# Mixture-of-experts stage of an encoder layer: the experts' instructions in a written order, eight split pairs, and the experts' inputs in another part of the memory

## The chip, the cores and the metric

The kernel runs on one core of a Trainium2 chip. The metric is the device time of one execution in microseconds (us). The kernel before takes 2306.76 us, the median of three runs (2303.48 to 2307.94).

A core has a matrix engine (TensorE, PE in the profile; PEld is its weight load), a vector engine (DVE), a scalar engine (ACT), GpSimd (POOL), and SyncE (SP), which here only issues loads. Each runs its own list of instructions in order and waits for the others through semaphores. Sixteen DMA engines move data between HBM and the on-chip memory SBUF (128 partitions). Matmul results go to PSUM.

## The reference

One layer: a token mixer (attention and a gated linear recurrence), then experts. The change touches only the experts, which end the program:

```python
def expert_choice_ffn(h, w_router, w_gate, w_up, w_down):
    ...
    affinity = jax.nn.softmax(logits, axis=-1)
    top_w, top_idx = lax.top_k(affinity.transpose(0, 2, 1), cap)
    xe = jax.vmap(lambda hb, ib: hb[ib])(h, top_idx)
    hid = jax.nn.silu(jnp.einsum('becd,edf->becf', xe, w_gate)) * jnp.einsum('becd,edf->becf', xe, w_up)
    ye = jnp.einsum('becf,efd->becd', hid, w_down) * top_w[..., None].astype(h.dtype)
    combine = lambda yb, ib: jnp.zeros((S, D), h.dtype).at[ib.reshape(-1)].add(yb.reshape(-1, D))
    return jax.vmap(combine)(ye, top_idx)
```

There are 16 experts. Each takes 128 of 1024 tokens of width 1024 and has a hidden width of 2048. All is float32.

## The kernel before

**Splitting.** A float32 product is made of three fp32r products. Every operand is split into a high part (a cast on ACT, line 89) and the rest (a subtraction on DVE, line 90), and `hi*hi + hi*lo + lo*hi` is summed in PSUM. The helper is `split`.

**Units.** The experts' weights come in units of 128 rows by 1024 columns (512 KB). A unit is loaded by SP (line 56) into a raw buffer (`er`), split into a pair `eh`, `el`, and used by six matmuls of 128 x 512. An expert has 48 units: for each of two halves of the hidden width, 8 of the gate matrix, 8 of the up matrix, 8 of the down matrix. In all there are 768 units and 4608 such matmuls.

**Matmuls.** For gate and up (`wide`, lines 1255 to 1257, into the PSUM tiles `pg`) the stationary operand is a 128 x 128 slice of the expert's transposed input, `xh` or `xl`; the moving operand is `eh` or `el`. For down (`down`, lines 1218 to 1220, into `py`) it is a slice of the transposed hidden rows, `hh` or `hl`.

**Between them.** `pick` (lines 1198 to 1206) makes the list of an expert's tokens: a one-hot tile `oh` on DVE, eight small matmuls, `idx` and `tw` on DVE, and a gather `xg` by a GpSimd DMA. `trans` turns a tile by PE (line 1184) and splits it: the input `xg` in eight pieces on ACT (line 1188, `xh`) and DVE (line 1189, `xl`), the hidden rows `hd` in two (`hh`, `hl` on lines 89 and 90). Silu is on ACT (line 1273), its product with up on DVE (line 1284), the weighting of the result (`ye`, line 1225) on DVE, and a GpSimd DMA adds it to the output (line 1226).

**What sets the order.** The order in which each engine's instructions stand is found by a scheduler that goes by priorities and its own estimates; the code is written gate, down of the half before, up. Nothing in the experts' part fixes it, except that a few splits are held back at the start.

**Buffers.** There are 26 raw buffers (7 `er`, 16 of a pool shared with earlier stages, 3 `er3`) and four more tiles (`ahead`) that are lent to loads before their own use starts. There are five pairs (`EB`), so a split waits until PE has used the unit five before it. SBUF is filled from both sides: pool `exr`, `side="right"`, holds `er`, `er3`, `ye` and the inputs `xh`, `xl`; pool `ex` on the left holds `hh`, `hl`, `xg`, `hd`; `ex1` holds the pairs. In the built program, counted in KB from the start of a partition: the pairs at 86 to 126, `hh` and `hl` at 146 to 154, `xh` and `xl` at 170 to 186. In PSUM, `pg` has banks 2 to 5, `py` 6 and 7; `s` of lines 928 to 930 has 2 to 4. In an earlier stage, lines 928 to 930, the stationary weights lie at 82 to 114 and the moving operands `och`, `ocl` at 134 to 198.

Of the kernel before, what the change touches and what calls it, by code (L numbers as in the profile page):

```python
# [21 lines left out]
P = 128  # L22
D = 1024
# [14 lines left out]
def trunk(ctx, tc, t, out, dbg=None):  # L38
# [16 lines left out]
    def load(dst, src):  # L55
        return nc.sync.dma_start(dst, src)
# [90 lines left out]
    def h4(name, shape, dt=F32R):  # L147
        return hpool.tile(shape, dt, name=name, tag="H", bufs=16)
# [993 lines left out]
    psE = ctx.enter_context(tc.tile_pool(name="psE", bufs=1, space=PSUM))  # L1142
    wg_, wu_, wd_ = (t[n].rearrange("l e a b -> (l e) a b") for n in ("w_exp_gate", "w_exp_up", "w_exp_down"))

    NR = ER + 16 + E3
    cnt = [0]
    held, ahead = [], []

    def eunit(src):
        shape = [P] + list(src.shape)[1:]  # L1150
        j = cnt[0] if cnt[0] < NR else cnt[0] - len(ahead)
        c = j % NR
        if NR <= cnt[0] < NR + len(ahead):
            raw = ahead[cnt[0] - NR]
        elif c < ER:
            raw = exr.tile(shape, F32, name="er", bufs=ER)
        elif c >= ER + 16:
            raw = exr.tile(shape, F32, name="er3", tag="er3", bufs=E3)
        else:
            raw = h4("er2", shape, F32)  # L1160
        if not NR <= cnt[0] < NR + len(ahead):
            load(raw, src)
        cnt[0] += 1
        hi = ex1.tile(shape, F32R, name="eh", bufs=EB)
        lo = ex1.tile(shape, F32R, name="el", bufs=EB)
        with ExitStack() as es:
            if cnt[0] <= EB:
                es.enter_context(tc.issue_after(first5[-2]))
                es.enter_context(tc.issue_after(first5[-1]))
            if 3 < cnt[0] <= 24:  # L1170
                es.enter_context(tc.issue_after(held[0]))
            if EB < cnt[0] <= 24:
                es.enter_context(tc.issue_after(held[8]))
            split(raw, hi, lo, nc.gpsimd if cnt[0] <= 3 else None)
        return hi, lo

    def trans(src, n, tag):
        pool = exr if tag == "x" else ex
        hi = pool.tile([P, n, P], F32R, name=tag + "h", tag=tag + "h", bufs=2)
        lo = pool.tile([P, n, P], F32R, name=tag + "l", tag=tag + "l", bufs=2)  # L1180
        for g in range(0, n, 4):
            p = psE.tile([P, 4, P], F32, name="tp", bufs=2)
            for c in range(4):
                nc.tensor.transpose(p[:, c], src[:, (g + c) * P:(g + c + 1) * P], ident)
            if tag == "x":
                for c in range(4):
                    k = g + c
                    held.append(nc.scalar.activation(hi[:, k], p[:, c], AF.Identity, bias=mcT[:, k:k + 1], scale=1.0).ins)  # L1188
                    nc.vector.scalar_tensor_tensor(lo[:, k], p[:, c], mcT[:, k:k + 1], hi[:, k].bitcast(F32),  # L1189
                                                   op0=ALU.add, op1=ALU.subtract)  # L1190
            else:
                split(p, hi[:, g:g + 4], lo[:, g:g + 4])
        return hi, lo

    def pick(e):

        oh = ex.tile([P, NT, P], BF16, name="oh", bufs=1)
        nc.vector.tensor_tensor(oh, slots[:, None, :].to_broadcast([P, NT, P]),
                                slot[:, :, e:e + 1].to_broadcast([P, NT, P]), ALU.is_equal)
        pi = psE.tile([P, 512], F32, name="tp", bufs=2)  # L1200
# [4 lines left out]
        xg = ex.tile([P, D], F32, name="xg", tag="xg", bufs=2)  # L1205
# [4 lines left out]
    def down(e, fp, hTs, py, ks):  # L1210

        for kk in ks:
            hh, hl = hTs[kk // 4]
            r = kk % 4
            wh, wl = eunit(dunit(e, (fp * 8 + kk) * P))
# [5 lines left out]
        if fp == 1 and ks[-1] == 7:  # L1221
            ye = exr.tile([P, D], F32, name="ye", tag="ye", bufs=YB)
            for n in range(2):
                sl = slice(n * 512, (n + 1) * 512)
                nc.vector.scalar_tensor_tensor(ye[:, sl], py[:, n], tw[:, e:e + 1], g2b[:, sl], op0=ALU.mult, op1=ALU.mult)
            nc.gpsimd.indirect_dma_start(out=out, out_offset=bass.IndirectOffsetOnAxis(ap=idx[:, e:e + 1], axis=0),
                                         in_=ye, in_offset=None, compute_op=ALU.add)

    def gunit(e, w, fp, k):
        return w[e, k * P:(k + 1) * P, fp * 1024:(fp + 1) * 1024].rearrange("(k p) n -> p k n", p=P)  # L1230
# [1 line left out]
    def dunit(e, r0):  # L1232
        return wd_[e, r0:r0 + P].rearrange("(k p) n -> p k n", p=P)


    for tag, n, src in (("ye", YB, dunit(0, 2 * P)), ("xh", 2, dunit(0, 3 * P)), ("xl", 2, dunit(0, 4 * P)),
                        ("xg", 2, dunit(0, 5 * P))):
        a = (exr if tag in X2 else ex).tile([P] + list(src.shape)[1:], F32, name="ahead", tag=tag, bufs=n)
        load(a, src)
        ahead.append(a)  # L1240

    with tc.high_priority(300):
        xparts = trans(pick(0), KT, "x")

    def wide(e, w, fp, parts, between=None):

        xh, xl = parts
        ps = [psE.tile([P, 512], F32, name="pg", bufs=4) for _ in range(2)]
        for k in range(KT):
            if between and k == 4:  # L1250
                between()
            wh, wl = eunit(gunit(e, w, fp, k))
            for n in range(2):
                sl = slice(n * 512, (n + 1) * 512)
                nc.tensor.matmul(ps[n], xh[:, k], wh[:, 0, sl], start=k == 0, stop=False)  # L1255
                nc.tensor.matmul(ps[n], xh[:, k], wl[:, 0, sl], start=False, stop=False)  # L1256
                nc.tensor.matmul(ps[n], xl[:, k], wh[:, 0, sl], start=False, stop=k == KT - 1)  # L1257
        return ps

    def turned(hds):  # L1260
        return [trans(hd, 4, "h") for hd in hds]

    pend = None
    py = None
    for e in range(NE):
        mine = xparts
        for fp in range(2):
            turn = []
            gs = wide(e, wg_, fp, mine, (lambda: turn.extend(turned(pend[2]))) if pend else None)
            acts = []  # L1270
            for n in range(2):
                hd = ex.tile([P, 512], F32, name="hd", tag="hd", bufs=3)
                nc.scalar.activation(hd, gs[n], AF.Silu)
                acts.append(hd)
            last = e == NE - 1 and fp == 1
            if fp == 0 and e + 1 < NE:
                xg = pick(e + 1)
            if pend and not last:
                if pend[1] == 0:
                    py = psE.tile([P, 2, 512], F32, name="py", bufs=1)  # L1280
                down(pend[0], pend[1], turn, py, range(8))
            us = wide(e, wu_, fp, mine)
            for n in range(2):
                nc.vector.tensor_tensor(acts[n], acts[n], us[n], ALU.mult)
            if fp == 1 and e + 1 < NE:
                xparts = trans(xg, KT, "x")
            if last:
                py = psE.tile([P, 2, 512], F32, name="py", bufs=1)
                down(pend[0], pend[1], turn, py, range(4))
                t0 = trans(acts[0], 4, "h")  # L1290
                down(pend[0], pend[1], turn, py, range(4, 8))
                down(e, 1, [t0, trans(acts[1], 4, "h")], py, range(8))
            pend = (e, fp, acts)
# [43 lines left out]
```

## Time and profile before

| | us |
|---|---|
| median of 3 runs | 2306.76 |
| the profiled execution, its own time | 2305.64 |
| its span, first to last instruction | 2303.80 |
| first matmul of the experts (line 1255) starts | 1132.36 |
| last DMA of the experts is issued (line 1226) | 2293.95 |
| between the two | 1161.59 |

The page gives, per engine, the busy time over the whole span. The views by stretch of time (windows), by waits, and the timelines are read below. A busy PE is not a PE at its peak, since matmuls overlap in the record: how fast it goes is read from the distance between the starts of two matmuls, called the pitch here.

### The profile page before, as it was taken

What the parts mean: (1) busy time and instruction counts of PE and PEld (TensorE: products, weight loads), DVE (VectorE), ACT (ScalarE), POOL (GpSimd) and SP (SyncE); (2) the same over time, 40 slices, a digit from 0 to 9 for tenths busy, and PEclk for the clock granted to TensorE, in tenths of its full rate; (3) what the DMA queues carried; (4) which work ended last, traced back from release to release, by engine and by line L of the source; (5) the groups of instructions that cost most, each with busy time, mean ns of one, the idle gap of its engine ahead of it and who ended that gap; (6) DMA issues with size and microseconds to landing.
All of it is one profiled execution on the core that took longest, in us unless ns stands there. A gap on an engine that the chain in (4) does not pass through costs nothing.

```text
span 2303.8 us, 30740 instructions
## 1 busy us (share of the span) xinstructions
PE 2150.1 (93%) x10518; PEld 1718.9 (75%) x10518; DVE 1868.5 (81%) x2601; ACT 1383.3 (60%) x2051; POOL 363.9 (16%) x341
## 2 busy tenths in 40 slices
PE   5998888999999999998499999999999999999997
PEld 4775665788888768897377877778777777777776
DVE  7699998588756465728899999999888898888886
ACT  4657666544433122224477777777777776777675
POOL 5247666000000000005200000000100000000000
PEclk9999999999999999999699999999999999999999
DMA  8111111422231885458589999999999999999992
GB/s 290 58 40 38 38 37 33 142 89 78 97 96 65 257 280 177 136 181 284 181 325 385 365 360 362 369 381 372 338 352 360 367 352 364 354 347 369 355 337 85
DMA packets 208246, 546.84 MB, mean 237 GB/s; under 512 B 19589, under 2 KB 75429, under 8 KB 208090
## 3 DMA queue, kind: packets, MB, share of 16 engines
q1 hardware_dynamic: 185242, 495.08, 59.4%
q0 software_dynamic: 8416, 29.41, 4.5%
q10 hardware_dynamic: 14432, 20.39, 2.5%
q8 instruction: 82, 1.34, 0.2%
q14 instruction: 74, 0.61, 0.1%
HBM read 503.80 MB, written 41.01 MB: 236 GB/s over the span
## 4 chain that ended last, share of the span: by engine, by line
PE 68%; DVE 14%; issue 7%; DMA 5%; ACT 4%; POOL 1%; SPq 0%; ACTq 0%; POOLq 0%; DVEq 0%
PE pg L1256 9%; PE pg L1257 9%; PE pg L1255 9%; PE py L1219 5%; PE py L1220 5%; PE py L1218 4%; DVE Tl L90 3%; PE g L208 2%; PE g L210 2%; PE s L711 2%; PE g L209 2%; DMA wr<-in_ada_w 2%; DVE el L90 2%; DVE mx L567 2%; ACT eh L89 1%
## 5 line engine op out<-in xcount | busy, mean ns | idle before, releaser
L90 DVE TENSOR_TENSOR el<-er,eh 128x1024 fp32r<-128x1024 f32 x761 | 898.1, 1220 | 66.3 <-ACT eh L89 54.6
L89 ACT CAST eh<-er 128x1024 fp32r<-128x1024 f32 x764 | 780.2, 1052 | 144.2 <-PE pg L1257 102.4
L1256 PE MATMUL pg<-el,xh 128*128 128x512 f32 x1024 | 412.0, 403 | 8.6 <-DVE el L90 7.5
L1257 PE MATMUL pg<-eh,xl 128*128 128x512 f32 x1024 | 402.1, 397 | 0.3
L1255 PE MATMUL pg<-eh,xh 128*128 128x512 f32 x1024 | 367.6, 399 | 3.6 <-ACT xh L1188 3.4
L1256 PEld LDWEIGHTS pg<-el,xh 128*128 128x128 f32 x1024 | 192.5, 188 | 65.0 <-DVE el L90 21.7
L1255 PEld LDWEIGHTS pg<-eh,xh 128*128 128x128 f32 x1024 | 192.4, 188 | 53.5 <-ACT xh L1188 7.8
L1257 PEld LDWEIGHTS pg<-eh,xl 128*128 128x128 f32 x1024 | 191.3, 188 | 48.2 <-DVE xl L1189 7.4
L1219 PE MATMUL py<-el,hh 128*128 128x512 f32 x512 | 202.8, 396 | 7.6 <-DVE el L90 7.6
L1218 PE MATMUL py<-eh,hh 128*128 128x512 f32 x512 | 201.5, 394 | 0.8 <-ACT eh L89 0.5
L1220 PE MATMUL py<-eh,hl 128*128 128x512 f32 x512 | 199.8, 390 | 0.0
L208 PE MATMUL g<-hTh,wh 128*128 128x512 f32 x448 | 179.8, 401 | 5.0 <-ACT wh L89 2.9
L210 PE MATMUL g<-hTh,wl 128*128 128x512 f32 x448 | 179.6, 401 | 0.3 <-DVE wl L90 0.2
L209 PE MATMUL g<-hTl,wh 128*128 128x512 f32 x448 | 178.8, 399 | 0.0
L1206 POOL DMA_INDIRECT xg<-d_h,idx x16 | 29.1, 1821 | 804.4 <-DVE idx L1203 678.2
L90 DVE TENSOR_TENSOR Tl<-E,Th 128x512 fp32r<-128x512 f32 x128 | 134.2, 1071 | 2.2 <-ACT Th L89 2.1
L638 POOL TENSOR_TENSOR sum<-sum,E 128x512 f32<-128x512 f32 x84 | 128.2, 1526 | 25.4 <-ACT E L632 20.4
L1219 PEld LDWEIGHTS py<-el,hh 128*128 128x128 f32 x512 | 96.0, 188 | 35.7 <-DVE el L90 15.6
L1218 PEld LDWEIGHTS py<-eh,hh 128*128 128x128 f32 x512 | 96.1, 188 | 25.1 <-ACT eh L89 5.1
L228 ACT ACTIVATE stg<-g 128x512 f32<-128x512 f32 (+1 forms) x78 | 45.1, 578 | 109.3 <-PE g L210 70.1
L1220 PEld LDWEIGHTS py<-eh,hl 128*128 128x128 f32 x512 | 96.2, 188 | 18.8
L90 DVE TENSOR_TENSOR wl<-wr,wh 128x1024 fp32r<-128x1024 f32 x56 | 68.6, 1227 | 43.9 <-ACT wh L89 43.9
(336 smaller groups left out, 3912.3 us busy)
## 6 DMA issues: line engine op xcount, KB each, us to landing
er<-in_w_exp_gate SPq DMA_DIRECT2D x256, 512.0 KB
er<-in_w_exp_up SPq DMA_DIRECT2D x256, 512.0 KB
er<-in_w_exp_down SPq DMA_DIRECT2D x252, 512.0 KB
wr<-in_w_in SPq DMA_DIRECT2D x42, 512.0 KB
wr<-in_ada_w SPq DMA_DIRECT2D x32, 512.0 KB
d_sg<-stg ACTq DMA_DIRECT2D x32, 256.0 KB
sg<-d_sg SPq DMA_DIRECT2D x16, 512.0 KB
d_zq<-stg ACTq DMA_DIRECT2D x24, 256.0 KB
```

The source lines that it names most:

```text
L89: first = nc.scalar.copy(hi, src)
L90: (eng or nc.vector).tensor_tensor(lo, src, hi.bitcast(F32), ALU.subtract)
L208: nc.tensor.matmul(p, wh[:, k], xT(hTh, n, k), start=k == 0, stop=False)
L209: nc.tensor.matmul(p, wh[:, k], xT(hTl, n, k), start=False, stop=False)
L210: nc.tensor.matmul(p, wl[:, k], xT(hTh, n, k), start=False, stop=k == KT - 1)
L638: (nc.vector if j == NH - 1 else nc.gpsimd).tensor_tensor(a, acc, E, ALU.add)
L1218: nc.tensor.matmul(py[:, n], hh[:, r], wh[:, 0, sl], start=fp == 0 and kk == 0, stop=False)
L1219: nc.tensor.matmul(py[:, n], hh[:, r], wl[:, 0, sl], start=False, stop=False)
L1220: nc.tensor.matmul(py[:, n], hl[:, r], wh[:, 0, sl], start=False, stop=fp == 1 and kk == 7)
L1255: nc.tensor.matmul(ps[n], xh[:, k], wh[:, 0, sl], start=k == 0, stop=False)
L1256: nc.tensor.matmul(ps[n], xh[:, k], wl[:, 0, sl], start=False, stop=False)
L1257: nc.tensor.matmul(ps[n], xl[:, k], wh[:, 0, sl], start=False, stop=k == KT - 1)
```

## The change

The experts' part is written as a list (`script`) of units and of actions between them, and an in-order block keeps that order on PE, DVE and ACT. Gate comes first, then up, then the down of the half before. The turn of the hidden rows stands before the fifth up unit, `pick` and the turn of the next input before the fifth down unit. The split of a unit is put on ACT and DVE right after the unit whose pair it takes over (`ensure`).

The memory is laid out anew. Raw buffers: 26 for the first 26 units, then a ring of 19 (3 `er`, 16 shared); one tile is lent instead of four. The seven `er3` tiles serve as raw buffers once, then hold three further pairs, so there are eight. `xh`, `xl` move to the left pool: they now lie at 136 to 152 KB, `hh`, `hl` at 160 to 168, the three further pairs at 170 to 198. `hd` has four buffers instead of three, `xg` one instead of two.

```diff
-    ER, E3, EB, YB = 7, 3, 5, 1
+    EB, MORE, YB = 5, 3, 1
+    RAW = dict(er=3, er3=7)
...
+    TAGS = ["er"] * 3 + ["H"] * 16 + ["er3"] * 7
+    RING, PAIR = ["er"] * 3 + ["H"] * 16, "er3"
...
+    def pair_tag(j):
+        return PAIR if j >= PAIRS0 and (j - PAIRS0) % (EB + MORE) >= EB else None
...
-        pool = exr if tag == "x" else ex
-        hi = pool.tile([P, n, P], F32R, name=tag + "h", tag=tag + "h", bufs=2)
-        lo = pool.tile([P, n, P], F32R, name=tag + "l", tag=tag + "l", bufs=2)
+        hi = ex.tile([P, n, P], F32R, name=tag + "h", tag=tag + "h", bufs=2)
+        lo = ex.tile([P, n, P], F32R, name=tag + "l", tag=tag + "l", bufs=2)
...
+        if tag == "x":
+            for k in range(n):
+                held.append(nc.scalar.activation(hi[:, k], ps[k // 4][:, k % 4], AF.Identity, bias=mcT[:, k:k + 1],
+                                                 scale=1.0).ins)
+            for k in range(n):
+                nc.vector.scalar_tensor_tensor(lo[:, k], ps[k // 4][:, k % 4], mcT[:, k:k + 1], hi[:, k].bitcast(F32),
+                                               op0=ALU.add, op1=ALU.subtract)
...
+    for h in range(NH2):
+        e, fp = divmod(h, 2)
+        more = e + 1 < NE
+        for k in range(KT):
+            wide_unit(e, wg_, h, (h, 0), k)
+        act(lambda h=h: silu(h))
+        if more and not fp:
+            act(lambda e=e: set_(ohs, e + 1, lambda: onehot(e + 1)))
+        for k in range(KT):
+            if k == 4:
+                if h:
+                    act(lambda h=h: (turn(h - 1, 0), turn(h - 1, 1)))
...
+            wide_unit(e, wu_, h, (h, 1), k)
+        act(lambda h=h: gated(h))
+        for kk in range(8) if h else ():
+            if kk == 4 and more:
+                if fp:
+                    act(lambda e=e: set_(xparts, e + 1, lambda: trans(xgs[e + 1], KT, "x")))
+                else:
+                    act(lambda e=e: set_(xgs, e + 1, lambda: pick(e + 1, ohs[e + 1])))
...
+            down_unit(h - 1, kk)
...
+    def ensure(done):
+
+        while len(parts_) < len(srcs) and before[len(parts_)] < done:
+            parts_.append(eparts(eload(srcs[len(parts_)]), len(parts_)))
...
+    with in_order(ET.PE, ET.DVE, ET.Activation):
+        j = 0
+        for z, run in script:
+            if z is None:
+                run()
+            else:
+                ensure(j)
+                run(*parts_[j])
+                j += 1
```

On ACT before, in the second half of the experts, the casts of units (`eh<-er`) and the split of the turned hidden rows (`hh<-tp`, which needs PE's transposes) stand like this:

```order
L89 CAST eh<-er_17615 128x1024
L89 CAST eh<-er_17627 128x1024
L89 CAST eh<-er_17671 128x1024
L89 CAST eh<-er_17683 128x1024
L89 CAST eh<-er_17695 128x1024
L89 CAST hh<-tp 128x512 x2
L89 CAST eh<-er_17707 128x1024
L89 CAST eh<-er 128x1024 x6
L1273 ACTIVATE hd<-pg 128x512 x2
```

The cast ahead of `hh` takes a pair that PE frees three units before the transposes. Now, at a like place of ACT:

```order
L1294 ACTIVATE hd<-pg 128x512 x2
L89 CAST eh<-er_19855 128x1024
L89 CAST eh<-er_19869 128x1024
L89 CAST eh<-er_19881 128x1024
L89 CAST eh<-er_19893 128x1024
L89 CAST hh<-tp 128x512 x2
L89 CAST eh<-er_19923 128x1024
L89 CAST eh<-er_19935 128x1024
```

Silu (`hd<-pg`) stands where gate ends, `hh` four casts later, where PE's transposes stand four units later: the cast ahead of `hh` takes the pair of the last but one unit before the transposes.

On DVE before, where the next expert's input is split (`xl`), its pieces alternate with the rests of units (`el`):

```order
L1189 SCALAR_TENSOR_TENSOR xl<-tp,mcT,xh 128x128
L90 TENSOR_TENSOR el<-er_16736,eh 128x1024
L1189 SCALAR_TENSOR_TENSOR xl<-tp,mcT,xh 128x128
L90 TENSOR_TENSOR el<-er_16748,eh 128x1024
L1189 SCALAR_TENSOR_TENSOR xl<-tp,mcT,xh 128x128
L90 TENSOR_TENSOR el<-er_16765,eh 128x1024
```

Now, at such a place of DVE, the eight pieces stand together:

```order
L1299 TENSOR_TENSOR hd<-hd,pg 128x512 x2
L90 TENSOR_TENSOR el<-er_16226,eh 128x1024
L90 TENSOR_TENSOR el<-er_16239,eh 128x1024
L90 TENSOR_TENSOR el<-er_16251,eh 128x1024
L90 TENSOR_TENSOR el<-er,eh 128x1024
L1208 SCALAR_TENSOR_TENSOR xl<-tp,mcT,xh 128x128 x8
L90 TENSOR_TENSOR el<-er,eh 128x1024 x2
```

The block follows the product of silu and up (`hd<-hd,pg`) by four units.

## Rows read from the trace of the kernel before

**Rows 1.** The page: span, busy time of each engine and its instructions, and GB/s of the DMA engines in 40 equal slices of the span.

```profile
span 2303.8 us, 30740 instructions
PE 2150.1 (93%) x10518; PEld 1718.9 (75%) x10518; DVE 1868.5 (81%) x2601; ACT 1383.3 (60%) x2051; POOL 363.9 (16%) x341
GB/s 290 58 40 38 38 37 33 142 89 78 97 96 65 257 280 177 136 181 284 181 325 385 365 360 362 369 381 372 338 352 360 367 352 364 354 347 369 355 337 85
```

**Rows 2.** Windows, from one expert's result (line 1225) to the next one's; the first is the start. Columns: stretch, its length, busy time (and count) of PE, weight loads, DVE, ACT, POOL, then the granted share of TensorE's clock, the busy share of the DMA engines, GB/s.

```profile
1130.00:1219.00 89.00, 87.67 (x396) 70.26 (x397) 79.07 (x88) 70.21 (x84) 3.02 (x2) 0.97 0.84 302
1219.01:1290.25 71.24, 70.64 (x321) 56.41 (x321) 66.53 (x70) 56.33 (x64) 4.14 (x3) 1.00 0.99 368
...
1503.95:1575.20 71.25, 70.66 (x321) 56.38 (x321) 66.53 (x70) 56.35 (x64) 4.11 (x2) 1.00 0.99 374
...
1865.10:1938.46 73.36, 71.68 (x321) 56.16 (x320) 64.94 (x70) 53.95 (x65) 4.04 (x3) 1.00 0.98 359
...
2159.47:2233.69 74.22, 71.45 (x313) 56.09 (x312) 63.61 (x67) 54.03 (x65) 2.32 (x2) 1.00 0.96 344
2233.69:2293.95 60.26, 56.80 (x249) 44.72 (x248) 50.83 (x49) 37.34 (x41) 2.30 (x2) 1.00 0.39 139
```

**Rows 3.** PE's timeline in one expert: start, duration, engine, line, shape. From 1432.06 to 1446.52 there are 62 pitches of gate matmuls, from 1455.31 to 1464.15 there are 39 of down matmuls.

```profile
1432.06 0.39 PE L1255 MATMUL pg<-eh,xh 128*128 128x512 f32 x1
...
1446.52 0.40 PE L1257 MATMUL pg<-eh,xl 128*128 128x512 f32 x1
1446.76 1.03 PE L1184 MATMUL tp<-ident,hd 128*128 128x128 f32 x8
1447.55 0.48 PE L1255 MATMUL pg<-eh,xh 128*128 128x512 f32 x1
1447.87 0.40 PE L1256 MATMUL pg<-el,xh 128*128 128x512 f32 x1
...
1455.31 0.39 PE L1218 MATMUL py<-eh,hh 128*128 128x512 f32 x1
...
1464.15 0.40 PE L1255 MATMUL pg<-eh,xh 128*128 128x512 f32 x1
```

**Rows 4.** PE's timeline around a `pick`, as rows 3.

```profile
1144.50 0.40 PE L1257 MATMUL pg<-eh,xl 128*128 128x512 f32 x1
1144.74 0.36 PE L1202 MATMUL tp<-tq,oh 128*128 128x5 bf16 x8
...
1145.27 0.39 PE L1256 MATMUL pg<-el,xh 128*128 128x512 f32 x1
```

**Rows 5.** PE's timeline in the earlier stage with moving operands at 134 to 198 KB; 33 pitches lie between the two rows.

```profile
939.89 0.39 PE L928 MATMUL s<-och,wh 128*128 128x512 f32 x1
...
947.37 0.39 PE L928 MATMUL s<-och,wh 128*128 128x512 f32 x1
```

**Rows 6.** Waits in 1718 to 2085 us (five experts): who waited for whom, us in total, times, longest.

```profile
ACT hh L89 <- PE tp L1184: 40.5, 10, 4.1
...
DVE hd L1284 <- PE pg L1257: 17.8, 10, 2.3
...
PEld pg L1256 <- DVE el L90: 11.4, 18, 1.2
PEld py L1219 <- DVE el L90: 9.4, 17, 1.1
```

**Rows 7.** ACT's timeline at the place shown in the order above; in brackets the idle time before and what ended it.

```profile
1909.49 1.05 ACT L89 CAST eh<-er 128x1024 fp32r<-128x1024 f32 x1 [0.35 <-PE pg L1257]
1914.60 1.08 ACT L89 CAST hh<-tp 128x512 fp32r<-128x512 f32 x2 [4.05 <-PE tp L1184]
1915.56 6.74 ACT L89 CAST eh<-er 128x1024 fp32r<-128x1024 f32 x7
```

**Rows 8.** The weight load on PE that comes late after it.

```profile
1919.66 0.19 PEld L1256 LDWEIGHTS pg<-el,xh 128*128 128x128 f32 x1 [0.49 <-DVE el L90]
```

**Rows 9.** Waits in 1219 to 1575 us (five experts).

```profile
PEld pg L1257 <- DVE xl L1189: 6.0, 15, 0.5
PEld pg L1255 <- ACT xh L1188: 5.8, 10, 0.8
```

**Rows 10.** The DMA engines in one expert, 1432 to 1504 us: GB/s in 40 slices of 1.8 us, and the sum.

```profile
GB/s 421 416 405 262 271 366 426 401 419 416 403 414 405 410 407 414 410 407 410 410 410 410 405 421 385 376 321 216 273 264 398 335 250 303 325 323 266 348 348 416
DMA packets 7244, 26.43 MB, mean 367 GB/s; under 512 B 802, under 2 KB 802, under 8 KB 7239
```

**Rows 11.** SP's waits in 1219 to 1575 us: the loads wait for a raw buffer, which DVE frees.

```profile
SPq L56 <- DVE el L90: 229.9, 220, 2.1
```

**Rows 12.** Where raw buffers on either side are read, 1219 to 1575 us: shortest, median and longest subtraction, in ns.

```profile
L90 DVE TENSOR_TENSOR el<-er,eh x241: 1212/1224/1230, 1218.6 to 1574.8; 128x1024 fp32r<-128x1024 f32 x121
```

**Rows 13.** The first matmuls of the experts (seven pitches apart), the last one, and the last DMA.

```profile
1132.36 0.79 PE L1255 MATMUL pg<-eh,xh 128*128 128x512 f32 x1
...
1135.17 0.39 PE L1256 MATMUL pg<-el,xh 128*128 128x512 f32 x1
...
2291.83 0.39 PE L1220 MATMUL py<-eh,hl 128*128 128x512 f32 x1
...
2293.95 1.55 POOL L1226 DMA_INDIRECT out<-ye,idx  x1 [57.96 <-DVE ye L1225]
```

More of the change, by code (lines that the diff above doesn't have):

```diff
@@ L1004, in trunk @@
     best = {}
-    ER, E3, EB, YB = 7, 3, 5, 1
-    X2 = dict(er3=E3, ye=YB, xh=2, xl=2)
-    X2_TAGS = ("er3", "er3", "er3", "ye", "xh", "xl", "xh", "xl")
+    EB, MORE, YB = 5, 3, 1
+    RAW = dict(er=3, er3=7)
+    X2 = dict(er3=7, ye=YB)
+    X2_TAGS = ("er3",) * 7 + ("ye",)
+    TAGS = ["er"] * 3 + ["H"] * 16 + ["er3"] * 7
+    RING, PAIR = ["er"] * 3 + ["H"] * 16, "er3"
+    NR = len(TAGS)
+    PAIRS0 = NR
     exr = ctx.enter_context(tc.tile_pool(name="exr", bufs=1, side="right"))
@@ L1143, in trunk, with eload @@
     wg_, wu_, wd_ = (t[n].rearrange("l e a b -> (l e) a b") for n in ("w_exp_gate", "w_exp_up", "w_exp_down"))
-    NR = ER + 16 + E3
     cnt = [0]
     held, ahead = [], []
-    def eunit(src):
+    def eload(src):
         shape = [P] + list(src.shape)[1:]
[L1151 to L1158, printed above, removed]
-        else:
[L1160 to L1165, printed above, removed]
+        j = cnt[0]
+        cnt[0] += 1
+        if NR <= j < NR + len(ahead):
+            return ahead[j - NR]
+        tag = TAGS[j] if j < NR else RING[(j - NR - len(ahead)) % len(RING)]
+        raw = h4("er2", shape, F32) if tag == "H" else exr.tile(shape, F32, name=tag, bufs=RAW[tag])
+        load(raw, src)
+        return raw
@@ new lines, in pair_tag, with pair_before, eparts @@
+    def pair_tag(j):
+        return PAIR if j >= PAIRS0 and (j - PAIRS0) % (EB + MORE) >= EB else None
+    def pair_before(j):
+        if pair_tag(j):
+            same = [i for i in range(PAIRS0, j) if pair_tag(i)]
+            return same[-MORE] if len(same) >= MORE else -1
+        same = [i for i in range(j) if not pair_tag(i)]
+        return same[-EB] if len(same) >= EB else -1
+    def eparts(raw, j):
+        shape = list(raw.shape)
+        tag = pair_tag(j)
+        if tag:
+            hi, lo = (exr.tile(shape, F32R, name=n, tag=tag, bufs=RAW[tag]) for n in ("eh", "el"))
+        else:
+            hi, lo = (ex1.tile(shape, F32R, name=n, bufs=EB) for n in ("eh", "el"))
@@ L1166, in eunit @@
         with ExitStack() as es:
-            if cnt[0] <= EB:
+            if j < EB:
                 es.enter_context(tc.issue_after(first5[-2]))
                 es.enter_context(tc.issue_after(first5[-1]))
[L1170 to L1174, printed above, removed]
+                if j >= 3:
+                    es.enter_context(tc.issue_after(held[0]))
@@ L1175, in eunit @@
+            split(raw, hi, lo, nc.gpsimd if j < 3 else None)
         return hi, lo
     def trans(src, n, tag):
-        pool = exr if tag == "x" else ex
-        hi = pool.tile([P, n, P], F32R, name=tag + "h", tag=tag + "h", bufs=2)
-        lo = pool.tile([P, n, P], F32R, name=tag + "l", tag=tag + "l", bufs=2)
+        hi = ex.tile([P, n, P], F32R, name=tag + "h", tag=tag + "h", bufs=2)
+        lo = ex.tile([P, n, P], F32R, name=tag + "l", tag=tag + "l", bufs=2)
+        ps = []
         for g in range(0, n, 4):
@@ L1184, in trans, with onehot @@
                 nc.tensor.transpose(p[:, c], src[:, (g + c) * P:(g + c + 1) * P], ident)
[L1185 to L1192, printed above, removed]
+            ps.append(p)
+        if tag == "x":
[6 more added lines that the diff above has]
+        else:
+            split(ps[0], hi, lo)
         return hi, lo
-    def pick(e):
+    def onehot(e):
         oh = ex.tile([P, NT, P], BF16, name="oh", bufs=1)
@@ L1199, in pick @@
                                 slot[:, :, e:e + 1].to_broadcast([P, NT, P]), ALU.is_equal)
+        return oh
+    def pick(e, oh):
         pi = psE.tile([P, 512], F32, name="tp", bufs=2)
@@ L1204, in pick @@
         nc.vector.tensor_reduce(tw[:, e:e + 1], pi[:, 0:3], AX.X, ALU.add)
-        xg = ex.tile([P, D], F32, name="xg", tag="xg", bufs=2)
+        xg = ex.tile([P, D], F32, name="xg", tag="xg", bufs=1)
         nc.gpsimd.indirect_dma_start(out=xg, out_offset=None, in_=d_h2[:, :],
@@ L1208, in pick, with gunit, dunit, unit @@
         return xg
[L1210 to L1215, printed above, removed]
+    def gunit(e, w, fp, k):
+        return w[e, k * P:(k + 1) * P, fp * 1024:(fp + 1) * 1024].rearrange("(k p) n -> p k n", p=P)
+    def dunit(e, r0):
+        return wd_[e, r0:r0 + P].rearrange("(k p) n -> p k n", p=P)
+    for tag, n, src in (("ye", YB, gunit(0, wu_, 1, 2)),):
+        a = (exr if tag in X2 else ex).tile([P] + list(src.shape)[1:], F32, name="ahead", tag=tag, bufs=n)
+        load(a, src)
+        ahead.append(a)
+    script = []
+    def unit(src, run):
+        script.append((src, run))
+    def act(run):
+        script.append((None, run))
+    xparts, hds, hTs, pys, xgs, ohs, banks = {}, {}, {}, {}, {}, {}, {}
+    def wide_unit(e, w, h, key, k):
+        def run(wh, wl):
+            if k == 0:
+                banks[key] = [psE.tile([P, 512], F32, name="pg", bufs=4) for _ in range(2)]
+            xh, xl = xparts[e]
+            for n in range(2):
+                sl = slice(n * 512, (n + 1) * 512)
+                p = banks[key][n]
+                nc.tensor.matmul(p, xh[:, k], wh[:, 0, sl], start=k == 0, stop=False)
+                nc.tensor.matmul(p, xh[:, k], wl[:, 0, sl], start=False, stop=False)
+                nc.tensor.matmul(p, xl[:, k], wh[:, 0, sl], start=False, stop=k == KT - 1)
+        unit(gunit(e, w, h % 2, k), run)
+    def down_unit(h, kk):
+        e, fp = divmod(h, 2)
+        def run(wh, wl):
+            if fp == 0 and kk == 0:
+                pys[e] = psE.tile([P, 2, 512], F32, name="py", bufs=1)
+            py, (hh, hl), r = pys[e], hTs[h, kk // 4], kk % 4
             for n in range(2):
@@ L1220, in down @@
                 nc.tensor.matmul(py[:, n], hl[:, r], wh[:, 0, sl], start=False, stop=fp == 1 and kk == 7)
[L1221 to L1240, printed above, removed]
@@ L1242, in trunk @@
-    with tc.high_priority(300):
[L1243 to L1293, printed above, removed]
@@ new lines, in run @@
+            if fp == 1 and kk == 7:
+                ye = exr.tile([P, D], F32, name="ye", tag="ye", bufs=YB)
+                for n in range(2):
+                    sl = slice(n * 512, (n + 1) * 512)
+                    nc.vector.scalar_tensor_tensor(ye[:, sl], py[:, n], tw[:, e:e + 1], g2b[:, sl], op0=ALU.mult, op1=ALU.mult)
+                nc.gpsimd.indirect_dma_start(out=out, out_offset=bass.IndirectOffsetOnAxis(ap=idx[:, e:e + 1], axis=0),
+                                             in_=ye, in_offset=None, compute_op=ALU.add)
@@ new lines, in down_unit, with silu, gated, turn @@
+        unit(dunit(e, (fp * 8 + kk) * P), run)
+    def silu(h):
+        hds[h] = []
+        for n in range(2):
+            hd = ex.tile([P, 512], F32, name="hd", tag="hd", bufs=4)
+            nc.scalar.activation(hd, banks[h, 0][n], AF.Silu)
+            hds[h].append(hd)
+    def gated(h):
+        for n in range(2):
+            nc.vector.tensor_tensor(hds[h][n], hds[h][n], banks[h, 1][n], ALU.mult)
+    def turn(h, n):
+        hTs[h, n] = trans(hds[h][n], 4, "h")
+    def set_(d, k, f):
+        d[k] = f()
@@ new lines, in trunk @@
+    NH2 = 2 * NE
+    for h in range(NH2):
+        e, fp = divmod(h, 2)
+        more = e + 1 < NE
[9 more added lines that the diff above has]
+                else:
+                    act(lambda: set_(xgs, 1, lambda: pick(1, ohs[1])))
+            wide_unit(e, wu_, h, (h, 1), k)
[4 more added lines that the diff above has]
+                    act(lambda e=e: set_(xparts, e + 1, lambda: trans(xgs[e + 1], KT, "x")))
+                else:
+                    act(lambda e=e: set_(xgs, e + 1, lambda: pick(e + 1, ohs[e + 1])))
+            if kk in (4, 6) and h == NH2 - 1:
+                act(lambda n=kk // 2 - 2: turn(h, n))
+            down_unit(h - 1, kk)
@@ new lines, in trunk @@
+    for kk in range(8):
+        down_unit(NH2 - 1, kk)
+    srcs = [z for z, _ in script if z is not None]
+    parts_ = []
+    before = [pair_before(j) for j in range(len(srcs))]
+    def ensure(done):
+        while len(parts_) < len(srcs) and before[len(parts_)] < done:
+            parts_.append(eparts(eload(srcs[len(parts_)]), len(parts_)))
+    with tc.high_priority(300):
+        xparts[0] = trans(pick(0, onehot(0)), KT, "x")
+    ensure(0)
+    with in_order(ET.PE, ET.DVE, ET.Activation):
[3 more added lines that the diff above has]
+                run()
+            else:
+                ensure(j)
+                run(*parts_[j])
+                j += 1
```

## The prediction

> **What bounds the kernel now.** The page comes first: the experts fill the half of the span where the DMA engines move 340 to 380 GB/s, and PE is busy almost all the time [rows 1]. Busy time doesn't tell whether PE does useful work at its best pace, so the next view is the windows from one expert's result to the next [rows 2]. The reader is to see two regimes: 71.24 us for an expert early on, 73.36 us later, and over 74 at the end. The clock is granted in full in both, so it isn't the cause.
>
> The third view is PE's timeline, for the pitch [rows 3]. Gate: (1446.52 - 1432.06) / 62 = 233.2 ns. Down: (1464.15 - 1455.31) / 39 = 226.7 ns. Eight transposes: from 1446.52 to 1447.87 are 1.35 us, less two pitches of 0.233, so 0.88. A pick costs 1145.27 - 1144.50 less the same two, 0.30 [rows 4]. An expert's work is 192 matmuls of gate and up (44.77 us), 96 of down (21.76), three times eight transposes (2.65) and a pick (0.30): 69.48 us. The first regime waits 1.76 us beside it, the second 3.88.
>
> Where the waits come from is in the waits and ACT's timeline. In the second regime ACT stands idle 4.1 us at a time for PE's transposes (`hh`), ten times in five experts [rows 6]; the cast before it began at 1909.49, the next came after 1915.56 [rows 7], although PE had freed three more pairs. With five pairs the lead is then gone: DVE comes late too and PE waits for `el` [rows 6, 8]. In the first regime the little that PE waits for is the next input, `xh` and `xl` [rows 9].
>
> The DMA engines look full (busy share 0.95 to 0.99 in these windows), but SP waits for a raw buffer in 230 of 356 us [rows 11], and in 30 us without an indirect transfer they hold 403 to 421 GB/s [rows 10]. So PE bounds, with waits that the order of ACT and DVE makes.
>
> **The change, part by part.** The whole stretch from the first matmul to the last DMA's issue is 2293.95 - 1132.36 = 1161.59 us [rows 13]. Its work is 16 x 69.48 = 1111.7, less the first expert's transposes and pick, which lie before it (1.2), plus the slow first pitches (2.81 for seven, where 1.63 would do: 1.2) and the end from the last matmul to the DMA's issue beyond one pitch (1.9): 1113.6. The waits are the other 48.0 us.
>
> *Order and pairs.* In the written order each split, silu and product stands behind the unit that frees or feeds it, so ACT and DVE never wait for something that PE does much later than what it has just ended. At `hh` ACT now waits for one unit and the transposes, some 2.2 us, while up to seven units lie ready with eight pairs; seven times 6 x 0.2267 are 9.5 us. Behind the waiting `hh` stand casts, and DVE's subtractions behind these; 9.5 us cover both. DVE's burst at the input is eight `xl` and a `ye`; it has to be under PE in the long run: 66.53 us busy in an expert [rows 2], under the 68.24 found below, and less when it runs back to back (64.94). What is left of the waits lies between nothing and the 1.76 of the first regime, the best that the old order did. Three things keep it off zero: DVE is within 3 us of PE, the loads within 2, and the start of an input still needs `xh` and `xl` at one moment. I take 0.6 us per expert, a third of the way, since eight pairs cover bursts that five nearly covered. So 48.0 become 9.6: 38.4 us less.
>
> *The inputs' place.* Gate and up differ from down in PSUM banks, in the moving tiles not at all, and in where the stationary tile lies: 170 to 186 KB against 146 to 154. Other matmuls of this shape, with stationary tiles at 82 to 114 KB and moving ones up to 198 KB, have the pitch of down: (947.37 - 939.89) / 33 = 226.7 ns [rows 5]. So I read the 6.5 ns as the price of a stationary tile in the right part. Moved to 136 to 152, where `hh` and `hl` were fast, `xh` and `xl` should run at 226.7: 3072 x 6.5 ns = 20.0 us less. An expert then has 288 x 0.2267 + 2.65 + 0.30 = 68.24 us of work. `hh` and `hl` move to 160 to 168, for which no row exists; its bounds are nothing and the same 6.5 ns on 1536 matmuls, 10.0 us. The fast row that is nearest ends at 154, 6 KB below; the slow one begins at 170, 2 KB above, but nothing says that the border is at its very edge. I take nothing, and keep the 10.0 as a case with a chance of its own.
>
> [...]
>
> *Pairs on the right.* Three of eight pairs are written and read at 170 to 198 KB. As moving operands they cost nothing [rows 5]; reading raw tiles on either side takes DVE 1212 to 1230 ns [rows 12]. Writing there has no row: between nothing and 2.9% (6.5 of 226.7) of 18 subtractions of 1.22 us, 0.6 us per expert on DVE, under its slack. I take nothing.
>
> *Fewer raw buffers.* 19 instead of 26, less some four in flight, are 15 units or 20 us of landed weights. The slowest stretch of rows 10, eleven slices (20 us) from 321 to 266 GB/s with a mean of 298, falls behind 384 GB/s by 20 x 86 / 384 = 4.5 us. They cover that, and the gather and the scatter, which now follow each other by four units. Cost nothing if so; the cover gone, it is a rival below. At the start fewer units are loaded early, but 26 and the first ring slots are there before 1132, which is 35 us of work. The single `xg` is read by the transposes half an expert before it is refilled: nothing. The new block of eight `xl` may make the first `xl` a little later: 0.8 us, once.
>
> Sum: -38.4 - 20.0 + 0.8 = -57.6, from 2305.64 to 2248.0 us. The profiled execution lies 1.1 us under the median and inside the range of the three runs, so no correction is made.
>
> **The rivals.**
>
> *The hidden rows turn slow at 160 to 168 KB.* For it: the border lies somewhere between 154 and 170. Against it: nothing but that. +10.0: 2258.
>
> *The place does nothing.* For it: gate and up also have other PSUM banks than down. Against it: the matmuls of rows 5 write to banks of `pg`, at the low pitch. +20.0: 2268.
>
> *The loads become the bound.* An expert moves 26.43 MB [rows 10]; at 68.84 us that is 384 GB/s, more than any window has (374 [rows 2]). If 374 is the most over an expert, it takes 70.67 us, 1.83 more than forecast, x 16 = 29: 2277. Against it: slices of 410 in rows 10, and SP's waits for buffers in both regimes.
>
> *Slower: the short ring can't hold the rate.* If loads, with 19 buffers, keep only the 359 GB/s of the second regime [rows 2], an expert takes 73.6 us, 4.8 more than forecast: 2324. The place is the stretch after gather and scatter, where PE would wait for a load at each expert; it decides from 4.2 us of waits per expert on, below 365 GB/s. For it: 359 was held for 370 us. Against it: there the loads waited for pairs, not for the memory. The Trainium skill (SBUF — State Buffer, A bandwidth-pool intuition that's wrong) gives about 358 GB/s from HBM to a core and calls HBM almost always the bound; by it nothing could be gained. The first regime, at 368 to 374 over five experts, speaks against it.
>
> *The change doesn't do what it says.* If the waits come from what the order does not touch, 2306. Against it: they sit at `hh`, `hd` and `xl`, which it moves.
>
> **How the numbers follow.** Forecast 0.46, hidden rows slow 0.17, place without effect 0.14, loads at 374 GB/s 0.13, short ring 0.06, no effect 0.03, faster than 2238 0.01. The forecast's own range is 2238 (no waits left) to 2255 (1.0 us each). The range for 8 in 10 goes from 2237 to 2278 and takes in the second, the third and the middle of the fourth case. 0.2%, 4.6 us, is about what a measurement of this kernel can tell from no change. Faster 0.91, same 0.03, slower 0.06.
>
> **What would show it.** In the profile after: experts 68.5 to 69.3 us apart in the windows; gate and up with a pitch of 226.7 ns; no idle stretch of 4 us on ACT before `hh`; DVE 94% busy and over; 380 GB/s and more. A gate pitch of 233 proves the place wrong, a down pitch of 233 the second case. Waits of PE or ACT for a DMA in each expert would make it wrong on the loads.

## The result and the profile after

The kernel after takes 2249.36 us, the median of four runs (2247.07 to 2252.45); the kernel before, 2307.35 (four runs). The ratio is 0.9753, its 95% interval 0.9736 to 0.9770. The forecast was 2248.0. The profiled execution took 2252.45 us. One of the four executions of the run with 64 bytes in the right pool, below, took 3659.93 us at a mean granted clock of 0.655, where the others had 0.985, and is left out.

The page of the kernel after, as [rows 1] of before:

```profile
span 2250.6 us, 30859 instructions
PE 2118.7 (94%) x10518; PEld 1729.7 (77%) x10518; DVE 1867.0 (83%) x2601; ACT 1370.3 (61%) x2051; POOL 365.3 (16%) x341
GB/s 296 59 37 42 37 40 27 117 111 84 86 93 68 197 278 231 146 165 207 205 214 390 387 380 378 388 373 389 379 377 388 375 383 382 380 383 381 374 386 105
```

PE is busy for 31 us less, DVE as long as before. The windows from one expert's result to the next, columns as in [rows 2]:

```profile
1299.57:1368.51 68.94, 68.94 (x321) 56.68 (x320) 65.67 (x70) 54.06 (x64) 4.09 (x2) 1.00 1.01 379
1851.18:1920.14 68.96, 68.96 (x321) 56.68 (x320) 65.69 (x70) 54.08 (x64) 4.11 (x3) 1.00 1.01 381
2126.99:2195.61 68.62, 68.62 (x313) 56.56 (x312) 64.58 (x67) 54.10 (x64) 2.32 (x1) 1.00 1.01 380
```

The two regimes are gone: an expert takes 68.95 us from the first window to the second (the last one shown, 68.62, has no next input to pick and turn), and PE is busy for the whole window. The forecast was 68.84. Waits over 1718 to 2085 us, as in [rows 6]:

```profile
ACT eh L89 <- PE pg L1266: 40.6, 86, 1.6
ACT hh L89 <- PE tp L1201: 8.5, 11, 0.8
DVE el L90 <- ACT eh L89: 6.0, 13, 0.7
```

ACT's 4.1 us at `hh` have become 0.8, and PE waits neither for `el` nor for `xl` or `xh`. What ACT waits for now is mostly a pair that PE is about to free (`eh`, 40.6 us in five experts): it keeps up.

So far all is as forecast. The pitch is not. PE's timeline in one expert: eight units, 48 pitches, from 1848.46 to 1859.45 (gate), and four units of down. The units from 1848.46 to 1851.21 and from 1858.06 on use right pairs, as do those from 1871.33 to 1874.08; the others use left pairs:

```profile
1848.46 0.39 PE L1264 MATMUL pg<-eh,xh 128*128 128x512 f32 x1
...
1851.21 0.40 PE L1264 MATMUL pg<-eh,xh 128*128 128x512 f32 x1
...
1853.98 0.39 PE L1264 MATMUL pg<-eh,xh 128*128 128x512 f32 x1
...
1858.06 0.40 PE L1264 MATMUL pg<-eh,xh 128*128 128x512 f32 x1
...
1859.45 0.39 PE L1264 MATMUL pg<-eh,xh 128*128 128x512 f32 x1
...
1871.33 0.39 PE L1278 MATMUL py<-eh,hh 128*128 128x512 f32 x1
...
1874.08 0.40 PE L1278 MATMUL py<-eh,hh 128*128 128x512 f32 x1
...
1879.11 0.39 PE L1278 MATMUL py<-eh,hh 128*128 128x512 f32 x1
...
1881.83 0.40 PE L1278 MATMUL py<-eh,hh 128*128 128x512 f32 x1
```

With right pairs, in the two units shown: 2.75 / 12 = 229 ns. The two units behind them, on left pairs: 2.77 / 12 = 231. The next three: 4.08 / 18 = 226.7. The first unit on the right again: 1.39 / 6 = 232. The mean over the eight is 10.99 / 48 = 229.0, where 226.7 was forecast. Down shows the same: 229 with right pairs, 2.72 / 12 = 226.7 with left ones. The stationary tiles lie in the left part for all of these, so that can't be what sets the pitch.

### The profile page after: what moved, and what is told of

Its sections match the earlier page's. It is cut to its first block, busy times and chain, and to the rows that moved or that the text cites. A ratio compares the mean times of both kernels' runs of the same rounds, so it can differ in the third digit from the quotient of the medians.

```text
span 2250.6 us, 30859 instructions
## 1 busy us (share of the span) xinstructions
PE 2118.7 (94%) x10518; PEld 1729.7 (77%) x10518; DVE 1867.0 (83%) x2601; ACT 1370.3 (61%) x2051; POOL 365.3 (16%) x341
## 3 DMA queue, kind: packets, MB, share of 16 engines
q8 instruction: 82, 1.34, 0.2%
## 4 chain that ended last, share of the span: by engine, by line
PE 73%; DVE 11%; DMA 6%; issue 5%; ACT 3%; POOL 1%; SPq 0%; ACTq 0%; POOLq 0%; DVEq 0%
PE pg L1264 10%; PE pg L1266 10%; PE pg L1265 10%; PE py L1278 5%; PE py L1280 5%; PE py L1279 5%; DVE Tl L90 4%; DMA wr<-in_ada_w 2%; PE g L208 2%; PE g L210 2%; PE s L711 2%; PE g L209 2%; PE tp L1201 2%; DVE mx L567 2%; PE s L930 1%
## 5 line engine op out<-in xcount | busy, mean ns | idle before, releaser
L90 DVE TENSOR_TENSOR el<-er,eh 128x1024 fp32r<-128x1024 f32 x764 | 897.0, 1219 | 43.8 <-ACT eh L89 20.2
L1264 PE MATMUL pg<-eh,xh 128*128 128x512 f32 x1024 | 405.8, 396 | 0.0
L1265 PE MATMUL pg<-el,xh 128*128 128x512 f32 x1024 | 399.4, 390 | 0.0
L228 ACT ACTIVATE stg<-g 128x512 f32<-128x512 f32 (+1 forms) x78 | 45.1, 578 | 112.4 <-PE g L210 84.8
```

The costliest lines, as they stand in the source:

```text
L90: (eng or nc.vector).tensor_tensor(lo, src, hi.bitcast(F32), ALU.subtract)
L1264: nc.tensor.matmul(p, xh[:, k], wh[:, 0, sl], start=k == 0, stop=False)
L1265: nc.tensor.matmul(p, xh[:, k], wl[:, 0, sl], start=False, stop=False)
```

## The experiments

What differs between the two kinds of unit is an address. The addresses are those of the built program. Pools on the left put their tiles at 64 bytes past a multiple of 256 (85.5625 KB, 135.5625 KB, 159.5625 KB), the right pool at 128 past one (170.125 KB). In the kernel before, gate and up had a stationary tile on the right and moving ones on the left; down and the matmuls of [rows 5] had both at remainder 64. Theory A: the pitch is set by whether the two addresses agree. Theory B is the prediction's: a stationary tile in the right part is slow. Some bytes of unused memory tell them apart.

**64 bytes in the right pool of the kernel after.**

```diff
+    exr.tile([P, 16], F32, name="pad")
```

> The kernel after, with 64 bytes of unused memory at the end of the right pool, so that everything in it lies 64 bytes lower. Then the three right pairs have the same address modulo 512 bytes (64) as the left pairs, xh, xl, hh and hl. Nothing else changes. Theory A (alignment): a matmul runs at 226.7 ns where its stationary and its moving tile agree in that remainder, and slower where they don't, wherever they lie. All 288 pitches of an expert fall from a mean of 228.8 to 226.7, an expert from 68.95 to about 68.35 us, and the time from 2249.4 by some 9.7. In the earlier stage (lines 928 to 930) the moving operands och and ocl are shifted as well, out of agreement with wh; by A its 384 matmuls go from 226.7 to 229 to 233, 1 to 2.5 us more: together 2241 to 2243. Theory B (place, that of the prediction: a tile in the right part costs): 64 bytes change no part, 2249, pitches as in the kernel after.

Measured: 2240.04 us (2236.26 to 2242.22), ratio to before 0.9715 (0.9694 to 0.9737). A window, and PE's timeline over two units with right pairs:

```profile
1838.68:1906.99 68.31, 68.31 (x322) 56.70 (x321) 65.56 (x70) 54.11 (x64) 4.10 (x2) 1.00 1.01 382
```

```profile
1846.81 0.39 PE L1265 MATMUL pg<-eh,xh 128*128 128x512 f32 x1
...
1849.53 0.39 PE L1265 MATMUL pg<-eh,xh 128*128 128x512 f32 x1
```

2.72 / 12 = 226.7 ns with right pairs too: A. One premise was wrong: `och` and `ocl` kept their addresses, and their matmuls their pitch, so the 1 to 2.5 us did not appear.

**The same in the kernel before.** The same line, ahead of the lent tiles.

> The kernel before, with the same 64 bytes: xh and xl stay in the right part (170 to 186 KB) but agree with the pairs in the remainder. A: gate and up fall from 233.3 to 226.7 ns; 3072 x 6.6 ns = 20 us less where PE bounds, less of it where ACT and DVE make PE wait: 2287 to 2300, with 1 to 2.5 us of the earlier stage in it. B: 2307 and a pitch of 233.3.

Measured: 2291.93 us, 0.9943 (0.9925 to 0.9961). A window of each regime, and 30 pitches of gate and up:

```profile
1498.87:1569.00 70.13, 69.53 (x322) 56.37 (x321) 66.38 (x70) 56.41 (x64) 4.11 (x2) 1.00 1.00 377
1855.65:1928.33 72.68, 70.89 (x321) 56.15 (x320) 64.95 (x70) 53.96 (x65) 4.04 (x2) 1.00 0.98 363
```

```profile
1434.13 0.39 PE L1256 MATMUL pg<-eh,xh 128*128 128x512 f32 x1
...
1440.93 0.39 PE L1256 MATMUL pg<-eh,xh 128*128 128x512 f32 x1
```

6.80 / 30 = 226.7 ns with `xh` still in the right part: B falls. An expert could have lost 192 x 6.6 ns = 1.27 us; it lost 1.11 in the first regime and 0.68 in the second. The rest, 0.16 and 0.59 us, went into waits: an expert's time beyond its work grew by as much.

**64 bytes on the left instead.** In the kernel after, ahead of `slot`, `ex1.tile([P, 16], F32, name="pad")`.

> The kernel after, with 64 bytes of unused memory at the start of the left pool ex1, so that the left pairs, xh, xl, hh and hl lie 64 bytes higher and agree with the right pairs (remainder 128 modulo 512, for all). The earlier stage keeps its addresses. A: 226.7 ns for all, 2239 to 2241. If it is not agreement that counts but the left tiles' remainder itself (64 good, 128 bad): all pitches slow, 228 to 233, 2249 to 2265. B: 2249.

Measured: 2240.58 us, 0.9714 (0.9698 to 0.9730).

```profile
1846.39:1914.71 68.32, 68.32 (x322) 56.66 (x321) 65.56 (x70) 54.04 (x64) 4.10 (x2) 1.00 1.01 384
```

Remainder 128 is as good as 64, as long as all have it.

**The written order alone.**

```diff
-    EB, MORE, YB = 5, 3, 1
-    RAW = dict(er=3, er3=7)
+    EB, MORE, YB = 5, 0, 1
+    RAW = dict(er=7, er3=3)
...
+        pool = exr if tag == "x" else ex
+        hi = pool.tile([P, n, P], F32R, name=tag + "h", tag=tag + "h", bufs=2)
+        lo = pool.tile([P, n, P], F32R, name=tag + "l", tag=tag + "l", bufs=2)
```

> The written order alone: five pairs, 26 raw buffers, xh and xl in the right part without agreement, as before; only hd has four buffers and xg one. Theory O (the order alone takes the waits away, the pairs add nothing): an expert takes its work, 69.5 us, plus some tenths, the time is 2305.6 - 48 + 16 x 0.2 = 2258 to 2262. Theory P (eight pairs are needed to cover the bursts at hh and xl): waits of 1 us and more per expert remain, 2275 or more, and PE waits for DVE's el.

Measured: 2262.42 us, 0.9820 (0.9801 to 0.9839). One thing more differs from the kernel before: one tile is lent to early loads, as in the kernel after, instead of four. A window, waits over 1718 to 2085 us, 60 pitches of gate and up, the first two units of a down block behind up, and the first and the last matmul of the experts:

```profile
1853.22:1922.87 69.65, 69.65 (x321) 56.69 (x321) 65.75 (x70) 55.46 (x64) 4.11 (x3) 1.00 1.00 377
```

```profile
DVE el L90 <- ACT eh L89: 14.0, 60, 0.7
ACT hh L89 <- PE tp L1202: 8.6, 11, 0.8
```

```profile
1850.47 0.40 PE L1265 MATMUL pg<-eh,xh 128*128 128x512 f32 x1
...
1864.47 0.40 PE L1265 MATMUL pg<-eh,xh 128*128 128x512 f32 x1
```

```profile
1839.23 0.40 PE L1279 MATMUL py<-eh,hh 128*128 128x512 f32 x1
...
1841.99 0.39 PE L1279 MATMUL py<-eh,hh 128*128 128x512 f32 x1
```

```profile
1129.84 0.79 PE L1265 MATMUL pg<-eh,xh 128*128 128x512 f32 x1
...
2244.22 0.39 PE L1281 MATMUL py<-eh,hl 128*128 128x512 f32 x1
```

The pitch is 14.00 / 60 = 233.3 ns, as before, and yet an expert takes 69.65 us, 0.17 over its work. PE waits for no split. Part of the 0.17 is pitch and not waits: the first two units of down behind up take 2.76 / 12 = 230 ns, and down's mean is 227.9, which is 96 x 1.2 ns = 0.1 us per expert. Theory O: the order takes nearly all waits away with five pairs. What is meant by the order is all that this run changes. The fourth `hd`, the single `xg` and the lent tiles were not varied by themselves (in the kernel before, no silu is seen to wait for a free `hd`), nor was the place of `hh` without the block of `xl`.

**Order and agreement, five pairs.** The order alone and the 64 bytes in the right pool.

> The written order with five pairs, 26 raw buffers and xh, xl in the right part (as in the run of the order alone), and the 64 bytes that make xh and xl agree with the pairs. If agreement and order are all that the change gave, and neither the eight pairs nor the place anything: gate and up fall from 233.3 to 226.7, an expert from 69.65 to 69.65 - 192 x 0.0066 = 68.4 us, the time from 2262.4 to 2242, the same as eight pairs that agree (2240). If eight pairs were needed once PE is faster: 69 us and more per expert, waits of PE for el, 2250 or more.

Measured: 2239.80 us (five runs), 0.9708 (0.9695 to 0.9722).

```profile
1843.49:1911.80 68.31, 68.31 (x322) 56.68 (x321) 65.56 (x70) 55.56 (x64) 4.11 (x3) 1.00 1.01 384
```

The expert takes as long as with eight pairs that agree, 68.31 us. The three further pairs, the shorter ring and the inputs' new place, taken together, gave nothing once the addresses agree.

**The inputs back on the right, eight pairs.** The last three added lines of the order's diff, in the kernel after, in place of its `hi` and `lo` lines in the left pool.

> The kernel after with xh and xl back in the right pool (186 to 202 KB, remainder 128), three pairs also there (154 to 182), five pairs, hh and hl on the left (remainder 64). A (alignment): gate and up at 226.7 with the right pairs and 233.3 with the left ones, some pitches between them after a change of side; down at 226.7 with left pairs, and slow with the right ones, as in the kernel after (228.8). B (place of the stationary tile): gate and up at 233.3 with every pair, down at 226.7 with every pair.

One execution: 2256.46 us. Gate with left pairs (30 pitches), then with a right pair (6):

```profile
1853.20 0.39 PE L1265 MATMUL pg<-eh,xh 128*128 128x512 f32 x1
...
1860.20 0.39 PE L1265 MATMUL pg<-eh,xh 128*128 128x512 f32 x1
...
1862.94 0.39 PE L1265 MATMUL pg<-eh,xh 128*128 128x512 f32 x1
1864.30 0.39 PE L1265 MATMUL pg<-eh,xh 128*128 128x512 f32 x1
```

7.00 / 30 = 233.3 and, in the third unit behind the change of side, 1.36 / 6 = 226.7, with one and the same stationary tile, as A has it. The two units between take 2.74 / 12 = 228 ns on the mean. Down has it the other way round, as A has it too: 226.7 with left pairs, 229 with right ones.

**How far apart is apart?** The kernel after with 32, 128, 192 and 320 bytes in the right pool, one execution of each. The address of the right pairs less that of the stationary tiles is then, modulo 256 bytes, +32, -64, +128 and 0; for 320 bytes it is a whole 256.

> As that run, with 32 bytes: right tiles at remainder 96 modulo 128, left ones at 64. If every difference within 128 bytes costs: right pairs slow, about 69 us per expert. If only which of two 64-byte halves a row of the tile starts in counts: 96 and 64 lie in the same half, 226.7 ns and 68.3 us.

> As the run with 64 bytes in the right pool, with 128: the right tiles have remainder 0 modulo 512, the moving tile is 64 bytes below the stationary one (in the kernel after it is 64 above). If the difference alone sets the pitch: 233.3 ns with the right pairs, as gate and up had in the kernel before, where the difference was the same with the sides exchanged; 69.1 us per expert. If only the amount of it counts: 228.8 ns, 68.95 us, as in the kernel after.

> As the run with 64 bytes in the right pool, with 192: the right tiles have remainder 64 modulo 128, as the left ones, but 448 modulo 512 and 192 modulo 256 where the left ones have 64. If the modulus that counts is 128: all at 226.7 ns, 68.3 us per expert. If it is 256 or 512: pitches with the right pairs slow, as in the kernel after or otherwise, about 69 us.

> As that run, with 320 bytes: right tiles at remainder 320 modulo 512, 256 bytes from the left ones. If the modulus that counts is 256: 226.7 ns, 68.3 us per expert. If it is 512: slow with the right pairs, 68.9 to 69.2 us.

Times: 2254.65, 2253.83, 2249.59 and 2238.51 us. PE's timeline over two units with right pairs, in the same order:

```profile
1849.36 0.39 PE L1265 MATMUL pg<-eh,xh 128*128 128x512 f32 x1
...
1852.16 0.39 PE L1265 MATMUL pg<-eh,xh 128*128 128x512 f32 x1
```

```profile
1848.55 0.39 PE L1265 MATMUL pg<-eh,xh 128*128 128x512 f32 x1
...
1851.35 0.39 PE L1265 MATMUL pg<-eh,xh 128*128 128x512 f32 x1
```

```profile
1844.89 0.40 PE L1265 MATMUL pg<-eh,xh 128*128 128x512 f32 x1
...
1847.69 0.39 PE L1265 MATMUL pg<-eh,xh 128*128 128x512 f32 x1
```

```profile
1849.23 0.39 PE L1265 MATMUL pg<-eh,xh 128*128 128x512 f32 x1
...
1851.95 0.39 PE L1265 MATMUL pg<-eh,xh 128*128 128x512 f32 x1
```

Three times 2.80 / 12 = 233.3 ns, and 2.72 / 12 = 226.7 for 256 bytes. So the difference of the two addresses (moving less stationary) modulo 256 bytes counts: 0 gives 226.7, +64 (the kernel after) 229, and +32, +128 and -64 (gate and up before) 233.3. For 0 and -64 this held with other remainders of the two as well; +32, +64 and +128 were seen with one pair of remainders each. The guesses that the modulus is 128, and that only the half of it counts, both fall.

**A short ring.** The edit makes the list of buffers ten entries long.

```diff
-    RING, PAIR = ["er"] * 3 + ["H"] * 16, "er3"
+    RING, PAIR = ["er"] * 3 + ["H"] * 7, "er3"
```

> The run with 64 bytes in the right pool, with the raw ring cut from 19 to 10 buffers. Loads land 17 to 20 us before their cast there; nine buffers less are nine units of 1.42 us, 12.8 us. If the ring is only a reserve, 4 to 7 us are left and nothing changes: 68.3 us per expert, 2240. If loads need a long ring to keep the rate (the short-ring case of the prediction): ACT waits for a DMA in each expert, 70 us and more, 2265 or more.

The edit does less than that. The 16 shared tiles are still used in turn, all of them, so there are 19 buffers as before; but the three `er` now come back every ten loads, and a load into one of them has to wait for the split of the unit ten before it. Over the experts, loads are issued 10 to 16 units ahead of the split, 11.7 on the mean, where they were 19 ahead in the run with 64 bytes.

One execution: 2245.75 us, with experts as fast as with loads 19 ahead. A window, and SP's waits over 1500 to 1850 us:

```profile
1848.09:1916.41 68.32, 68.32 (x322) 56.69 (x321) 65.57 (x70) 54.22 (x64) 4.11 (x2) 1.00 1.01 385
```

```profile
SPq L56 <- DVE el L90: 147.6, 72, 6.2
SPq L56 <- DMA er<-in_w_exp_down: 40.5, 40, 3.2
```

SP now waits for transfers as well, but neither ACT nor PE does. The 6 us over the run with 64 bytes are not the ring's: the experts only start later. The first matmul of them in the run with 64 bytes and here:

```profile
1128.42 0.79 PE L1265 MATMUL pg<-eh,xh 128*128 128x512 f32 x1
```

```profile
1138.16 0.79 PE L1265 MATMUL pg<-eh,xh 128*128 128x512 f32 x1
```

PE, ACT and DVE have the same instructions ahead of the experts in both, and the first load that goes elsewhere (the 38th) is issued behind that matmul, at 1150.7 us here. The delay comes up earlier: 2.6 of the 9.7 us are there at PE's 2000th matmul, at 470 us. In the other runs the start lies between 1128 and 1136 us; what moves it was not tried.

## Why the prediction was right, and where it was not

The number came out for the right reason in its larger term, and by two wrong sizes that cancel. That the median came within 1.4 us of the forecast is luck.

*Order and pairs, forecast -38.4.* The mechanism was the one named: waits at `hh` that hold up the casts behind them. The order alone, with the old pitch, takes the time from the first matmul to the last from 2291.83 - 1132.36 = 1159.5 us to 1114.4 (1129.84 to 2244.22), 45.1 less. The step that was mis-sized is "I take 0.6 us per expert" for the waits that are left: they are 0.17 at most. ACT waits 0.8 us at `hh`, not 2.2, and DVE's block of `xl` delays nobody. The part "and pairs" of that term was wrong: with five pairs the order does the same, so the 9.5 us of cover were not needed.

*The inputs' place, forecast -20.0.* Here the step failed that read "I read the 6.5 ns as the price of a stationary tile in the right part". The experiments showed that the price is for addresses that differ modulo 256 bytes. In the prediction's own [rows 5] the two addresses agree, at remainder 64, and so these rows could not show that moving operands on the right "cost nothing". Moving `xh` and `xl` to the left brought them into agreement with the left pairs, and three of eight pairs out of it. From the order alone to the kernel after the stretch falls from 1114.4 to 2238.46 - 1134.94 = 1103.5 us, 10.9 less instead of 20:

```profile
1134.94 0.79 PE L1264 MATMUL pg<-eh,xh 128*128 128x512 f32 x1
...
2238.46 0.40 PE L1280 MATMUL py<-eh,hl 128*128 128x512 f32 x1
```

The pitches account for 3072 x (233.3 - 229.0) ns = 13.2 us gained by gate and up and, with down's mean at 227.9 in the order alone and 229.1 in the kernel after, 1536 x 1.2 ns = 1.8 lost by down, which the forecast had at nothing. (The means of down are over units without transposes or a pick among them.) That makes 11.4, 0.5 us more than was measured over the 16 experts, which stays unexplained.

*The sum.* Forecast -58.4 for the two, measured -56.0. With 0.43 us per expert too much of waits and some 0.6 too little of pitch, 68.84 against 68.95 us looks better than its parts are. The profiled execution lies 53.2 us under that of before, since its experts began 2.6 us later (1134.94 against 1132.36); the +0.8 for the first `xl` can't be told from that scatter.

*Fewer raw buffers, forecast nothing.* Right: 19 do, and in one execution a lead of 10 to 16 units did as well. The rival with loads at 374 GB/s falls, since 379 to 385 were held over experts, and so does the short ring. The Trainium skill (SBUF — State Buffer, A bandwidth-pool intuition that's wrong) has about 358 GB/s from HBM to a core; the windows above differ from it, and the measurement decides. The prediction took the 368 to 374 of the first regime as speaking against that figure, but these count the gather and the scatter. SP's loads alone, before (1432 to 1504 us) and after (1368 to 1437 us), in packets, MB and share of the engines:

```profile
q1 hardware_dynamic: 6951, 25.32, 92.1%
...
q1 hardware_dynamic: 6916, 25.18, 95.2%
```

That is 352 GB/s before and 365 after. What spoke against the figure before the change were the 403 to 421 GB/s that [rows 10] show for 30 us, not the mean of an expert.

*The other rivals.* The hidden rows at 160 to 168 KB run at 226.7 ns with left pairs, so that place isn't slow either. "The place does nothing" was right in its title and wrong in its reason: the banks are the same in all these runs. The prediction's own list had as its sign a gate pitch of 233; 229 came, which fitted neither this rival nor the forecast.

## What to carry to other kernels

When two groups of equal matmuls have different pitches, compare the remainders of their operands' addresses modulo 256 bytes before their places or banks: 64 bytes of unused memory were worth 0.64 us per expert in the kernel after (68.95 to 68.31), 10 us in all, and 1.34 with the order alone (69.65 to 68.31), 21 in all. The fastest kernels, at 2240 us, are the written order with either five or eight pairs and such a pad. A wait of an in-order engine for something that a later unit produces holds up all that stands behind it; writing the order down removed 45 us, and more pairs were not needed for it. And when a forecast comes out right, check its terms one by one: here two were off by 7 and 9 us.

## What had not been expected of the hardware

The pitch of these fp32r matmuls of 128x512, each with a weight load of its own, depends on the difference of the two operands' addresses: 226.7 ns at a multiple of 256 bytes, 229 to 233.3 ns otherwise (+32, +64, +128 and -64 were seen). A change between the two takes a while: in the kernel after, the first twelve matmuls on left pairs behind right ones took 231 ns on the mean, and only then 226.7; with 32, 128 and 192 bytes in the right pool it was the first six, at 229 to 231. Matmuls of other shapes or types were not measured, and what in the chip makes this was not tried.
